# Rotating the token indexer's queries and keys in feature layout, with VectorE's shuffle in place of TensorE transposes

## Chip, cores and metric

The kernel runs on one core of one Trainium2 chip. The metric is the device time of one launch in microseconds (us), the median over repeated runs. Five engines run their own instruction streams: TensorE (PE, with its weight loads shown apart as PEld), VectorE (DVE), ScalarE (ACT), GpSimd (POOL) and SyncE (SP), whose queue here issues nearly all DMAs.

## Reference, cut to what matters

The reference is one encoder layer: RMSNorm, one input projection, two groups of attention heads, a gated output projection, a residual add. The change touches the indexer of group A, which scores keys for every query and lets each query keep its 128 best:

```python
q_i = q_i.reshape(B, S, IDX_HEADS, IDX_DIM)                       # 8 heads of 64
q_i = jnp.concatenate([rope(q_i[..., :IDX_ROPE_DIM], pos), q_i[..., IDX_ROPE_DIM:]], axis=-1)
k_i = jnp.concatenate([rope(k_i[..., :IDX_ROPE_DIM], pos), k_i[..., IDX_ROPE_DIM:]], axis=-1)
...
rel = jax.nn.relu(jnp.einsum('bqhd,bsd->bqhs', qib, k_idx))
score = jnp.einsum('bqhs,bqh->bqs', rel, wb) * idx_scale          # wb: w_i, one weight a head
```

`rope` turns the first 32 of 64 features: with halves x1, x2 of 16 features it gives x1·cos − x2·sin and x2·cos + x1·sin, an angle for each position. S is 512, the model width 1024, all values float32.

## The kernel before, in words

Every float32 operand of a matmul is split into a rounded part and a rest (`xh`, `xl` of the normed input; `wh`, `wl` of a weight chunk), and a product is three matmuls: high·high, high·low, low·high (`mm3`, L188). A weight chunk is 128 rows of a projection. `chunk` (L292) loads it (SP), ACT casts it to `wh` (L299), and POOL or DVE subtracts to `wl` (L302). The chunks stand in one list in the order of their use (L314 to L320), with three staging buffers behind the first eight chunks, so a load waits for the subtraction three chunks back. A letter per chunk says which engine subtracts: "PPPD" for the eight chunks of q_i, "P" for c_kv, "D" for c_q.

PE's order is that of the program text; that of the other engines comes from a scheduler and from explicit edges (`after`, L232; `first`, L257, which holds the casts of later chunks behind an instruction). `later` (L137) puts off a closure, such as a turn of finished rows by transposes, until so much PE time has been issued. `stream` (L342) runs several accumulations staggered by `skew` chunks, each in a PSUM bank of the tags named; the tags hold 3 (mm), 2 (tr), 2 (sc) and 1 (pv) banks.

The stretch around the change runs like this:

- The small projection (104 columns: the 32 rotary key columns of group B, then the 64 of `k_i`, then the 8 of `w_i`) accumulates feature by token in `sm_acc`, in between the first steps of q_i (L540 to L553).
- `use_small` (L456) copies it out, four transposes bring it to token layout, DVE rotates there with the table `cs32`, a second turn of four 128x128 transposes brings `k_i`, written twice side by side, back to feature layout, and `split` makes KIH and KIL.
- q_i is projected token by feature, for the token tiles 1 to 3 (tile 0 needs no scores): `tok_jobs` at L539, 3 jobs of 8 chunks of 3 matmuls, 128x512 each. `use_qi` (L566) rotates a finished tile on DVE (three operations of 128x256), and 3000 ns of PE time later four 128x128 transposes turn it, two casts on ACT and two subtractions on DVE fill the tiles QI (rounded part in one half of the partitions, rest in the other).
- `lkv` (L629) projects c_kv feature by token, 2 jobs of 8 chunks; after nine steps the index matmuls (L602, L603) come in between, two for each head and token tile, in the banks sc and tr by turns; ACT takes the relu, DVE adds it up with the weight of the head (L608, L610). Then comes c_q (`lq`, L630).
- `tables` (L425) multiplies, on POOL, the rotary tables with the gains of the head norms (TB for group B, TA for group A).

Of the kernel before, what the change touches and what calls it, by code (L numbers as in the profile page):

```python
# [88 lines left out]
def layer(ctx: ExitStack, tc: tile.TileContext, x, norm_gain, w_in, a_q_norm, a_k_norm, b_q_latent,  # L89
# [364 lines left out]
    QSUM = []  # L454

    def use_small(_, a):  # L456
        st = tmp()
        first(nc.scalar.copy(st[:104], a[:104]), KEEP_SMALL)

        def turn():  # L460
            p = psum("tr")
# [2 lines left out]
            nc.scalar.copy(sm.rearrange("p t c -> p (t c)"), p[:, :416])
            p3 = p[:, :416].rearrange("p (t c) -> p t c", t=NT)

            kid = tmp((128, NT, 128))
            k4 = kid.rearrange("p t (u d) -> p t u d", u=2)
            m = tmp((128, NT, 32))
            for u in range(2):  # L470
                nc.scalar.copy(k4[:, :, u, 32:64], p3[:, :, 64:96])
            src = p3[:, :, 32:64]
            nc.vector.tensor_tensor(halves(m), halves(src)[:, :, ::-1, :], halves(cs32[:, 1]), op=OP.mult)
            nc.vector.tensor_tensor(src, src, cs32[:, 0], op=OP.mult)
            for u in range(2):
                nc.vector.tensor_tensor(k4[:, :, u, 0:32], src, m, op=OP.add)
# [593 lines left out]
```

## Time and profile before

| what | value |
|---|---|
| median of 3 runs | 337.01 us (336.97 to 338.79) |
| the profiled execution's own time | 336.93 us |
| its span, first to last instruction | 335.2 us |
| what lies around the span | 1.7 us |
| instructions | 5486 |
| HBM read, written | 27.07 MB, 2.10 MB |

The time of an instruction in the profile is its busy time. Matmuls are pipelined, so one of 0.40 us can be followed by the next 0.23 us later: what a matmul costs is read from the distance of two starts. A number in brackets behind a row of the timeline is idle time of the engine just before, with what ended it; a row with x4 merges four instructions in a row.

### The profile page before, as it was taken

What the parts mean: (1) busy time and instruction counts of PE and PEld (TensorE: products, weight loads), DVE (VectorE), ACT (ScalarE), POOL (GpSimd) and SP (SyncE); (2) the same over time, 40 slices, a digit from 0 to 9 for tenths busy, and PEclk for the clock granted to TensorE, in tenths of its full rate; (3) what the DMA queues carried; (4) which work ended last, traced back from release to release, by engine and by line L of the source; (5) the groups of instructions that cost most, each with busy time, mean ns of one, the idle gap of its engine ahead of it and who ended that gap; (6) DMA issues with size and microseconds to landing.
All of it is one profiled execution on the core that took longest, in us unless ns stands there. A gap on an engine that the chain in (4) does not pass through costs nothing.

```text
span 335.2 us, 5486 instructions
## 1 busy us (share of the span) xinstructions
PE 327.5 (98%) x1691; PEld 274.2 (82%) x1691; DVE 261.2 (78%) x630; ACT 214.7 (64%) x530; POOL 183.7 (55%) x203
## 2 busy tenths in 40 slices
PE   7899999999999999999999999999999999999995
PEld 5788888888898988888888888888778788888884
DVE  4864779669998595778898989777997776878466
ACT  4925658683666677878877898434426988978210
POOL 3846543376899996135714579537734535745100
PEclk9999999999999999999999999999999999999999
DMA  7912344133133324014300354208977324420006
GB/s 277 356 35 62 98 119 135 45 104 95 44 93 94 101 83 131 1 36 124 77 19 1 88 140 134 80 0 191 228 178 230 91 75 141 127 64 1 2 0 250
DMA packets 28695, 34.77 MB, mean 104 GB/s; under 512 B 5357, under 2 KB 16762, under 8 KB 28666
## 3 DMA queue, kind: packets, MB, share of 16 engines
q1 hardware_dynamic: 25856, 32.45, 34.3%
q10 hardware_dynamic: 2810, 1.97, 2.3%
q8 instruction: 13, 0.21, 0.3%
q14 instruction: 16, 0.13, 0.1%
HBM read 27.07 MB, written 2.10 MB: 87 GB/s over the span
## 4 chain that ended last, share of the span: by engine, by line
PE 91%; DVE 3%; DMA 1%; issue 1%; POOL 1%; ACT 1%; SPq 0%; DVEq 0%; POOLq 0%
PE mm L130 54%; PE sc L130 12%; PE pv L130 11%; PE tr L134 6%; PE tr L130 5%; PE mm L134 2%; DVE ob L1025 2%; DMA xin<-in_x 1%; PE sc L134 1%; PE pv L134 1%; DVE xin L385 0%; POOL tmp L840 0%; POOL sml L227 0%; DVE mal L843 0%; DVE z L764 0%
## 5 line engine op out<-in xcount | busy, mean ns | idle before, releaser
L302 POOL TENSOR_TENSOR wl<-wst,wh 128x512 fp32r<-128x512 f32 (+2 forms) x80 | 100.4, 1264 | 47.9 <-ACT wh L299 43.3
L299 ACT CAST wh<-wst 128x512 fp32r<-128x512 f32 (+2 forms) x89 | 50.8, 589 | 23.7 <-DMA wst<-in_w_in 12.7
L130 PE MATMUL mm<-wh,xh 128*128 128x512 f32 x112 | 47.0, 420 | 0.0
L130 PE MATMUL mm<-wl,xh 128*128 128x512 f32 x112 | 44.4, 397 | 0.0
L130 PE MATMUL mm<-wh,xl 128*128 128x512 f32 x112 | 44.3, 395 | 0.0
L766 ACT ACTIVATE z<-z,sml 128x256 f32<-128x256 f32 (+2 forms) x64 | 35.9, 561 | 9.6 <-DVE sml L764 8.7
L795 POOL TENSOR_SCALAR z<-z,sml 128x512 f32<-128x512 f32 (+2 forms) x32 | 18.0, 561 | 42.8 <-DVE sml L791 30.5
L227 POOL TENSOR_TENSOR sml<-sml,nhalf 128x4 f32<-128x4 f32 (+2 forms) x28 | 31.6, 1130 | 14.9 <-ACT sml L918 13.7
L130 PE MATMUL mm<-xh,wh 128*128 128x512 f32 x88 | 36.7, 417 | 0.0
L130 PE MATMUL mm<-xl,wh 128*128 128x512 f32 x88 | 34.8, 395 | 0.0
L130 PE MATMUL mm<-xh,wl 128*128 128x512 f32 x88 | 34.7, 394 | 0.0
L621 DVE MAX8 m<-acc 128x8 f32<-128x512 f32 (+2 forms) x48 | 26.4, 551 | 0.0
L622 DVE MATCH_REPLACE8 acc<-m,acc 128x512 f32<-128x512 f32 (+2 forms) x48 | 25.9, 541 | 0.0
L130 PEld LDWEIGHTS mm<-wh,xl 128*128 128x128 f32 x112 | 21.1, 188 | 4.8
L130 PEld LDWEIGHTS mm<-wl,xh 128*128 128x128 f32 x112 | 21.2, 190 | 3.5 <-POOL wl L302 0.5
L130 PEld LDWEIGHTS mm<-wh,xh 128*128 128x128 f32 x112 | 21.1, 189 | 3.1 <-issue 0.2
L447 DVE TENSOR_TENSOR pl<-tr,ph 128x512 fp32r<-128x512 f32 (+1 forms) x32 | 17.6, 549 | 4.7 <-ACT ph L447 4.7
L764 DVE CUSTOM_DVE_ANT_0 z<-sc,wide,nqb 128x512 f32<-128x512 f32 (+3 forms) x32 | 17.3, 541 | 4.2 <-PE sc L130 4.0
L447 ACT CAST ph<-tr 128x512 fp32r<-128x512 f32 (+1 forms) x32 | 15.1, 472 | 8.5 <-PE tr L134 8.1
L130 PE MATMUL sc<-kl,bhl 96*128 96x512 f32 (+3 forms) x96 | 20.0, 320 | 0.0
L130 PEld LDWEIGHTS mm<-xh,wl 128*128 128x128 f32 x88 | 16.5, 188 | 4.0
L130 PEld LDWEIGHTS sc<-kl,bhl 96*128 96x128 f32 x96 | 16.7, 189 | 3.0
(248 smaller groups left out, 878.8 us busy)
## 6 DMA issues: line engine op xcount, KB each, us to landing
wst<-in_w_in SPq DMA_DIRECT2D x48, 256.0 KB, 2.7
wst<-in_w_out SPq DMA_DIRECT2D x16, 256.0 KB, 2.8
xin<-in_x SPq DMA_DIRECT2D x4, 512.0 KB, 4.8
ob<-in_x SPq DMA_DIRECT2D x8, 256.0 KB, 3.9
wst<-in_w_in SPq DMA_DIRECT2D x8, 192.0 KB, 2.4
wst<-in_w_uq SPq DMA_DIRECT2D x6, 192.0 KB, 2.6
wst<-in_w_in SPq DMA_DIRECT2D x8, 128.0 KB, 2.2
wst<-in_w_ukv SPq DMA_DIRECT2D x4, 256.0 KB, 2.8
```

The source lines that it names most:

```text
L130: nc.tensor.matmul(o, l, r, start=start, stop=stop)
L134: nc.tensor.transpose(o, i, idn)
L227: return nc.gpsimd.tensor_tensor(dst, src, nhalf[:, :src.shape[-1]], op=OP.pow)
L299: copies.append(nc.scalar.copy(h, st))
L302: i = E(eng).tensor_tensor(l, st, f32(h), op=OP.subtract)
L447: return nc.scalar.copy(h, p), nc.vector.tensor_tensor(l, p, f32(h), op=OP.subtract)
L621: nc.vector.max(m, masks[t])
L622: MR.append(nc.vector.match_replace(masks[t], m, masks[t], -3e38))
L764: m = nc.vector.tensor_tensor_reduce(z, sc[:, :n], mask(t), nq(h, t), 3e38, OP.add, OP.min, r[:, i:i + 1])
L766: e = nc.scalar.activation(z, z, AF.Exp, bias=r[:, i:i + 1], scale=-1.0, accum_out=r[:, 2 + i:3 + i])
L795: nc.gpsimd.tensor_scalar(z, z, w, 0.0, op0=OP.mult, op1=OP.add)
L1025: ADD[name, c, t] = nc.vector.tensor_tensor(o, p[:, :n], o, op=OP.add)
```

## The change

Queries and keys of the indexer never enter token layout.

- q_i is projected feature by token: `qi_jobs` makes four jobs (groups of 128 columns, two heads each) over the 384 tokens of the tiles 1 to 3, 8 chunks of 3 matmuls, 128x384 each, in the banks mm, mm, tr, sc.
- In that layout the two halves of a rotary pair lie 16 partitions apart in a block of 32. `use_qi` shuffles the bank's partitions by 16 within each block to SBUF (`stream_shuffle`, DVE), multiplies the bank in place with the cosines (DVE) and the shuffled copy with the signed sines (POOL), and adds the copy onto the bank (DVE). The casts and subtractions to QI read the bank; the 12 transposes of q_i are gone.
- `use_small` does the same with the 64 rows of `k_i`, which now lie first among the 104, and KIH and KIL are written twice from the bank; the second turn with its four transposes is gone, and the first turns only 40 rows (`w_i`, rotary keys of group B) instead of 104.
- Cosines and sines in feature layout are 1024 new columns of the constants, loaded in two DMAs of 256 KB (`turns`) on SP's queue, behind the table `cs32`. DVE's operand `turns[0]` is 1 and POOL's `turns[1]` 0 on the 32 features that do not turn.
- The subtractions of c_q's chunks go to POOL and DVE by turns. The products of `table` are put behind the last sine product on POOL. The edge that held KIL behind the last rotary sum of q_i falls away.

```diff
+    freqs = np.power(10000.0, -np.arange(16) * 2.0 / 32).astype(np.float32)
+    ang = (pos[None, :] * freqs[:, None]).astype(np.float64)
+    c, s = np.cos(ang), np.sin(ang)
+    head = np.stack([np.concatenate([c, c, np.ones((32, S))]), np.concatenate([-s, s, np.zeros((32, S))])], 1)
+    feat = np.concatenate([head, head]).reshape(128, -1).astype(np.float32)
...
+QI_SKEW = 1.99
+QI_BANK = "mm", "mm", "tr", "sc"
+QI_POOL = True
...
-        nc.sync.dma_start(wst[:, ks, 0:32], wv[:, ks, 3272:3304])
-        nc.sync.dma_start(wst[:, ks, 32:104], wv[:, ks, 2560:2632])
+        nc.sync.dma_start(wst[:, ks, 72:104], wv[:, ks, 3272:3304])
+        nc.sync.dma_start(wst[:, ks, 0:72], wv[:, ks, 2560:2632])
...
+    turns = [sb("pt2", (128, S), name=f"turns{i}") for i in range(2)]
...
-    weight("c_q", "D")
+    weight("c_q", "PD")
...
-        nc.gpsimd.tensor_tensor(dst[:, 0], raw[:, 0], g[:, None, :].to_broadcast([128, NT, d]), op=OP.mult)
+        after(nc.gpsimd.tensor_tensor(dst[:, 0], raw[:, 0], g[:, None, :].to_broadcast([128, NT, d]), op=OP.mult), SINE[-1])
...
     def use_small(_, a):
-        st = tmp()
-        first(nc.scalar.copy(st[:104], a[:104]), KEEP_SMALL)
+        st, m = tmp(), tmp()
+        first(nc.scalar.copy(st[64:104], a[64:104]), KEEP_SMALL)
+        w = sb("bq", (64, S))
+        nc.vector.stream_shuffle(w, a[0:64], [(i + 16) % 32 for i in range(32)])
+        nc.vector.tensor_tensor(a[0:64], a[0:64], turns[0][0:64], op=OP.mult)
+        nc.gpsimd.tensor_tensor(w, w, turns[1][0:64], op=OP.mult)
+        nc.vector.tensor_tensor(a[0:64], a[0:64], w, op=OP.add)
+        for u in range(2):
+            nc.scalar.copy(KIH[HALF[u]], a[0:64])
+        for u in range(2):
+            kil = nc.vector.tensor_tensor(KIL[HALF[u]], a[0:64], f32(KIH[0:64]), op=OP.subtract)
 
         def turn():
             p = psum("tr")
             for t in range(NT):
-                transpose(p[:, t * 104:t * 104 + 104], st[:104, tok(t)], ident[:104, :104])
+                transpose(p[:, t * 40:t * 40 + 40], st[64:104, tok(t)], ident[64:104, 64:104])
...
-            def turn2():
-                p = psum("tr")
-                for t in range(NT):
-                    transpose(p[:, tok(t)], kid[:, t], ident)
-                kil = split(KIH, KIL, p)[1]
-                if len(QSUM) == 3:
-                    after(kil, QSUM[2])
-            later(LAG_KI, turn2)
...
+    def qi_jobs():
+        def job(g):
+            def step(a, k):
+                h, l = wt("q_i", k)
+                mm3(a[:, :384], h[:, tok(g)], l[:, tok(g)], xh(k)[:, 128:], xl(k)[:, 128:], k == 0, k == 7)
+            return 8, step, lambda a: use_qi(g, a)
+        return [job(g) for g in range(4)]
...
-    qi_ = stream(tok_jobs("q_i", 8, xh, xl, 512, [1, 2, 3], lambda t, a: use_qi(t, a), mm3=mm3w), 3, ("mm", "mm", "pv"), 1.99)
+    qi_ = stream(qi_jobs(), 4, QI_BANK, QI_SKEW)
...
             nc.sync.dma_start(cs32, cst[:, 512:768])
+            for i in range(2):
+                nc.sync.dma_start(turns[i], cst[:, 1408 + i * S:1408 + i * S + S])
...
-    def use_qi(t, a):
-        q = tmp()
...
-        rope_mul(a3[:, :, 0:32], m, a3[:, :, 0:32], cs32, t, 8, 32)
-        QSUM.append(nc.vector.tensor_tensor(q3[:, :, 0:32], a3[:, :, 0:32], m, op=OP.add))
...
-            for h in range(4):
-                transpose(p[:, tok(h)], q[:, tok(h)], ident)
...
+    def use_qi(g, a):
+        w = sb("bq", (128, 384))
+        p = a[:, :384]
+        nc.vector.stream_shuffle(w, p, [(i + 16) % 32 for i in range(32)])
+        nc.vector.tensor_tensor(p, p, turns[0][:, 128:], op=OP.mult)
+        sine = (nc.gpsimd if QI_POOL else nc.vector).tensor_tensor(w, w, turns[1][:, 128:], op=OP.mult)
+        SINE.append(sine)
+        QSUM.append(nc.vector.tensor_tensor(p, p, w, op=OP.add))
+        for u in range(2):
+            nc.scalar.copy(QI[u][HALF[u], g], p[HALF[u]])
+        for u in range(2):
+            nc.vector.tensor_tensor(QI[u][HALF[1 - u], g], p[HALF[u]], f32(QI[u][HALF[u], g]), op=OP.subtract)
```

How the order moves on three engines. First PE, where q_i ends and c_kv begins (L134 is a transpose, `pv_355` the bank of the last q_i tile, `mm_514` that of c_kv). Before:

```order
L134 MATMUL tr_477<-ident_65,tmp_450 128x128 x4
L130 MATMUL pv_355<-wh_299,xh1_107 128x512
L130 MATMUL pv_355<-wh_299,xl1_109 128x512
L130 MATMUL pv_355<-wl_300,xh1_107 128x512
L130 MATMUL mm_514<-xh0_106,wh_310 128x512
L130 MATMUL mm_514<-xl0_108,wh_310 128x512
L130 MATMUL mm_514<-xh0_106,wl_311 128x512
L134 MATMUL tr_524<-ident_65,tmp_414 128x128 x4
L130 MATMUL mm_514<-xh0_106,wh_327 128x512
```

PE at the same place now (`tr_359` and `sc_419` are the banks of the third and fourth group of q_i, `mm_554` that of c_kv):

```order
L138 MATMUL tr_359<-xh1_109,wh_301 128x384
L138 MATMUL tr_359<-xl1_111,wh_301 128x384
L138 MATMUL tr_359<-xh1_109,wl_302 128x384
L138 MATMUL sc_419<-xh1_109,wh_295 128x384
L138 MATMUL sc_419<-xl1_111,wh_295 128x384
L138 MATMUL sc_419<-xh1_109,wl_296 128x384
L138 MATMUL sc_419<-xh1_109,wh_301 128x384
L138 MATMUL sc_419<-xl1_111,wh_301 128x384
L138 MATMUL sc_419<-xh1_109,wl_302 128x384
L138 MATMUL mm_554<-xh0_108,wh_312 128x512
L138 MATMUL mm_554<-xl0_110,wh_312 128x512
L138 MATMUL mm_554<-xh0_108,wl_313 128x512
```

The turns between the projections are gone, and c_kv follows q_i directly; from the first index matmul on PE's order is the old one. Second DVE, from the second group of q_i to the last subtraction for QI (`qi0`, `qi1`), as it stands now; `kr` is the product of the group B keys with the table TB:

```order
L584 TENSOR_TENSOR mm_323<-mm_323,bq_490 128x384
L580 STREAM_SHUFFLE bq_526<-sc_419 128x384
L581 TENSOR_TENSOR sc_419<-sc_419,turns0_98 128x384
L584 TENSOR_TENSOR tr_359<-tr_359,bq_511 128x384
L588 TENSOR_TENSOR qi0_402<-mm_323,qi0_402 64x384
L588 TENSOR_TENSOR qi1_403<-mm_323,qi1_403 64x384
L588 TENSOR_TENSOR qi0_402<-tr_359,qi0_402 64x384
L588 TENSOR_TENSOR qi1_403<-tr_359,qi1_403 64x384
L311 TENSOR_TENSOR wl_576<-wst_573,wh_575 128x384
L584 TENSOR_TENSOR sc_419<-sc_419,bq_526 128x384
L691 TENSOR_TENSOR kr_904<-sm_155,tb1_151 128x128
```

Behind these stand one more subtraction for c_q and the two subtractions of the fourth group, ahead of the first accumulation of the index. Third POOL, from the sine product of the keys (L472) to the first of the queries (L582):

```order
L311 TENSOR_TENSOR wl_296<-wst_293,wh_295 128x512
L472 TENSOR_TENSOR bq_393<-bq_393,turns1_99 64x512
L311 TENSOR_TENSOR wl_313<-wst_310,wh_312 128x256
L311 TENSOR_TENSOR wl_330<-wst_327,wh_329 128x256
L311 TENSOR_TENSOR wl_349<-wst_346,wh_348 128x256
L311 TENSOR_TENSOR wl_369<-wst_366,wh_368 128x256
L582 TENSOR_TENSOR bq_463<-bq_463,turns1_99 128x384
```

The first four subtractions of c_kv stand ahead of the first sine product of the queries; the other three sine products come, one or two chunks apart, among the rest of c_kv and the first of c_q, and all of `table` behind the last.

More of the change, by code (lines that the diff above doesn't have):

```diff
@@ L40, in constants @@
     wide = np.concatenate([np.zeros((128, 384), np.float32), mask], 1)
+    freqs = np.power(10000.0, -np.arange(16) * 2.0 / 32).astype(np.float32)
[3 more added lines that the diff above has]
+    feat = np.concatenate([head, head]).reshape(128, -1).astype(np.float32)
     return np.ascontiguousarray(
-        np.concatenate([table(64), table(32), np.eye(128, dtype=np.float32), wide], 1))
+        np.concatenate([table(64), table(32), np.eye(128, dtype=np.float32), wide, feat], 1))
 AHEAD = 8
@@ L414, in table @@
         h = d // 2
-        nc.gpsimd.tensor_tensor(dst[:, 0], raw[:, 0], g[:, None, :].to_broadcast([128, NT, d]), op=OP.mult)
+        after(nc.gpsimd.tensor_tensor(dst[:, 0], raw[:, 0], g[:, None, :].to_broadcast([128, NT, d]), op=OP.mult), SINE[-1])
         for a, b in ((0, h), (h, 0)):
-            nc.gpsimd.tensor_tensor(dst[:, 1, :, a:a + h], raw[:, 1, :, a:a + h],
-                                    g[:, None, b:b + h].to_broadcast([128, NT, h]), op=OP.mult)
+            after(nc.gpsimd.tensor_tensor(dst[:, 1, :, a:a + h], raw[:, 1, :, a:a + h],
+                                          g[:, None, b:b + h].to_broadcast([128, NT, h]), op=OP.mult), SINE[-1])
     TB = [P.tile([128, 2, NT, 32], F32, name=f"tb{i}") for i in range(2)]
@@ L462, in turn @@
             for t in range(NT):
-                transpose(p[:, t * 104:t * 104 + 104], st[:104, tok(t)], ident[:104, :104])
[L464 to L476, printed above, removed]
-            nc.scalar.activation(sm[:, :, 96:104], sm[:, :, 96:104], AF.Copy, scale=512 ** -0.5)
-            def turn2():
-                p = psum("tr")
-                for t in range(NT):
-                    transpose(p[:, tok(t)], kid[:, t], ident)
-                kil = split(KIH, KIL, p)[1]
-                if len(QSUM) == 3:
-                    after(kil, QSUM[2])
-            later(LAG_KI, turn2)
+                transpose(p[:, t * 40:t * 40 + 40], st[64:104, tok(t)], ident[64:104, 64:104])
+            p3 = p[:, :160].rearrange("p (t c) -> p t c", t=NT)
+            nc.scalar.copy(sm, p3)
+            nc.scalar.activation(sm[:, :, 0:8], sm[:, :, 0:8], AF.Copy, scale=512 ** -0.5)
         later(LAG_SMALL, turn)
@@ L564, in layer @@
     QI = [sb("qk8", (128, 4, 384), F32R, f"qi{u}") for u in range(2)]
-    def use_qi(t, a):
-        q = tmp()
-        q3 = q.rearrange("p (h d) -> p h d", h=8)
-        m = tmp((128, 8, 32))
-        a3 = a.rearrange("p (h d) -> p h d", h=8)
-        first(nc.scalar.copy(q3[:, :, 32:64], a3[:, :, 32:64]), KEEP_QI)
-        rope_mul(a3[:, :, 0:32], m, a3[:, :, 0:32], cs32, t, 8, 32)
-        QSUM.append(nc.vector.tensor_tensor(q3[:, :, 0:32], a3[:, :, 0:32], m, op=OP.add))
-        def turn():
-            p = psum("tr" if t == 1 else "sc")
-            for h in range(4):
-                transpose(p[:, tok(h)], q[:, tok(h)], ident)
-            p3 = p.rearrange("p (h c) -> p h c", h=4)
-            for u in range(2):
-                nc.scalar.copy(QI[u][HALF[u], :, tok(t - 1)], p3[HALF[u]])
-            for u in range(2):
-                a, b = QI[u][HALF[u], :, tok(t - 1)], QI[u][HALF[1 - u], :, tok(t - 1)]
-                nc.vector.tensor_tensor(b, p3[HALF[u]], f32(a), op=OP.subtract)
-        later(LAG_QI, turn)
+    def use_qi(g, a):
[10 more added lines that the diff above has]
+            nc.vector.tensor_tensor(QI[u][HALF[1 - u], g], p[HALF[u]], f32(QI[u][HALF[u], g]), op=OP.subtract)
     run(qi_)
```

9 lines of the change are left out of this document (5 added, 4 removed).

## Prediction

> **What bounds the kernel now.** I read the page first: the busy shares, the granted clock, the chain that ended last.
>
> ```profile
> PE 327.5 (98%) x1691; PEld 274.2 (82%) x1691; DVE 261.2 (78%) x630; ACT 214.7 (64%) x530; POOL 183.7 (55%) x203
> PEclk9999999999999999999999999999999999999999
> PE 91%; DVE 3%; DMA 1%; issue 1%; POOL 1%; ACT 1%; SPq 0%; DVEq 0%; POOLq 0%
> ```
>
> PE is busy for 98% of the span at the full granted clock, and the chain runs over it for 91%. A busy PE is not yet a PE without holes, so I read the stages next.
>
> ```profile
> core 0: us, PE busy (x) PEld busy (x) DVE busy (x) ACT busy (x) POOL busy (x), PEclk, DMA share, GB/s
> 15.00:36.00 21.00, 21.00 (x103) 17.09 (x103) 11.23 (x21) 9.34 (x25) 10.84 (x10) 1.00 0.26 76
> 36.00:50.00 14.00, 14.00 (x69) 11.36 (x68) 11.66 (x19) 9.27 (x20) 8.02 (x17) 1.00 0.44 119
> 50.00:130.00 80.00, 80.00 (x387) 67.95 (x386) 65.24 (x169) 53.28 (x139) 60.45 (x66) 1.00 0.32 91
> 130.00:250.00 120.00, 119.95 (x651) 100.85 (x650) 103.53 (x248) 80.27 (x195) 62.85 (x56) 1.00 0.38 92
> 250.00:305.00 55.00, 54.46 (x302) 46.02 (x301) 41.25 (x123) 45.31 (x116) 28.09 (x31) 1.00 0.39 116
> ```
>
> From 15 to 250 us PE is without a visible hole. So the time is PE's list of work plus what it waits for: PE work taken out between 15 and 50 us, where the change lies, shortens the run one for one, and a new wait of PE lengthens it one for one. Work on DVE and POOL costs only where it makes PE wait.
>
> **Part 1, the turns that go.** PE's timeline around one turn (start, busy time, what):
>
> ```profile
> 36.54 0.39 PE L130 MATMUL mm<-xh,wl 128*128 128x512 f32 x1
> 36.77 0.60 PE L134 MATMUL tr<-ident,tmp 128*128 128x128 f32 x4
> 37.12 0.48 PE L130 MATMUL mm<-xh,wh 128*128 128x512 f32 x1
> 37.44 0.40 PE L130 MATMUL mm<-xl,wh 128*128 128x512 f32 x1
> 37.68 0.40 PE L130 MATMUL mm<-xh,wl 128*128 128x512 f32 x1
> ```
>
> The four transposes hold PE from 36.77 to 37.12, 0.35 us. The matmul behind them takes 0.32 to the next start, where the one after it takes 0.24: 0.08 more. A turn costs 0.43 us. All such transposes of this stretch (34 to 41 us):
>
> ```profile
> L134 PE MATMUL tr<-ident,tmp x8: 272/273/273, 34.9 to 37.1; 128*128 128x128 f32 x8
> L134 PE MATMUL sc<-ident,tmp x8: 272/273/274, 37.9 to 40.1; 128*128 128x128 f32 x8
> ```
>
> Sixteen of one length, so four turns (three of q_i, the second of `k_i`): 4 × 0.43 = 1.72 us out.
>
> The first turn of the small projection stays, with 40 columns for 104:
>
> ```profile
> 27.55 0.52 PE L134 MATMUL tr<-ident,tmp 104*128 104x104 f32 x4
> 27.84 0.48 PE L130 MATMUL mm<-wh,xh 128*128 128x512 f32 x1
> 28.16 0.39 PE L130 MATMUL mm<-wh,xl 128*128 128x512 f32 x1
> ```
>
> It takes 0.29 us for 416 columns; by columns 160 take 0.11, by instructions still 0.29. The turn above had 512 columns in 0.35, nearly in proportion, so I take 0.12 us out, between 0 and 0.18.
>
> **Part 2, q_i in other tiles.** 72 matmuls of 512 columns become 96 of 384, the same 36,864 columns. Both widths side by side:
>
> ```profile
> 89.74 0.39 PE L130 MATMUL mm<-xh,wh 128*128 128x512 f32 x1
> ...
> 90.44 0.34 PE L130 MATMUL sc<-wh,lath 128*128 128x384 f32 x1
> ...
> 91.49 0.39 PE L130 MATMUL mm<-xh,wh 128*128 128x512 f32 x1
> ```
>
> Three of 512 take 0.70 us (89.74 to 90.44), then six of 384 take 1.05 (to 91.49): 0.233 and 0.175 each. 72 × 0.233 = 16.8 and 96 × 0.175 = 16.8: nothing.
>
> [...]
>
> **Part 3, the operands at q_i's start.** The steps are shorter, so each chunk is wanted earlier, and POOL and DVE make them no faster:
>
> ```profile
> 13.52 3.81 POOL L302 TENSOR_TENSOR wl<-wst,wh 128x512 fp32r<-128x512 f32 x3
> 18.88 3.29 DVE L538 TENSOR_TENSOR swl<-smw,swh 128x416 fp32r<-128x416 f32 x2
> 15.88 0.39 PE L130 MATMUL mm<-wh,xh 128*128 128x512 f32 x1
> 22.89 2.00 PE L130 MATMUL mm<-xh,swl 128*104 128x512 f32 x8
> ```
>
> The second chunk began at 15.88; now the first step is 0.17 shorter, so at 15.71, and its third matmul, which reads the rest, at 16.06: the second of POOL's three ends at 13.52 + 2/3 × 3.81 = 16.06. The low products of the small projection, behind nine steps, move from 22.89 to 22.89 − 9 × 0.175 = 21.31; their second half wants DVE's second instruction (done 22.17) at 21.31 + 4 × 0.23 = 22.23. Both just fit, with no room for the way of a signal. I take 0.1 us lost, between 0 and 0.3. SP's queue gets the two loads of `turns` behind that of `cs32`:
>
> ```profile
> 12.37 0.41 SPq L551 DMA_DIRECT2D cs<-cst  x1
> 13.05 0.33 SPq L295 DMA_DIRECT2D wst<-in_w_in  x1
> 28.58 4.68 SPq L295 DMA_DIRECT2D wst<-in_w_in  x5
> 36.23 0.33 SPq L427 DMA_DIRECT2D tmp<-cst  x1
> ```
>
> Two issues at the 0.68 us between these first two set the next rows back by 1.4 us, while the five loads at 28.58 wait for staging buffers anyway; and `turns` is wanted only behind the small projection, after 23 us. The load of the raw table (36.23) now stands ahead of those five; its buffer held only squares of the input norm, done long before, so it goes at once. Cost nothing; if it did wait, the c_kv loads would, and with them POOL's list in part 4.
>
> **Part 4, the long chain on DVE and POOL.** Neither a shuffle nor a sine product is in this trace; the nearest rows, by form:
>
> ```profile
> L573 DVE TENSOR_TENSOR tmp<-mm,tmp 128x256 f32<-128x256 f32 x2 | 0.8, 424 | 0.1
> L584 DVE TENSOR_TENSOR qi<-sc,qi 64x512 fp32r<-64x512 f32 x4 | 2.8, 688 | 0.1
> L302 DVE TENSOR_TENSOR wl<-wst,wh 128x384 fp32r<-128x384 f32 x5 | 3.2, 654 | 1.5 <-ACT wh L299 1.4
> L688 DVE TENSOR_TENSOR kr<-sm,tb 128x128 f32<-128x128 f32 x1 | 0.9, 909 | 0.0
> L302 POOL TENSOR_TENSOR wl<-wst,wh 128x384 fp32r<-128x384 f32 x6 | 6.1, 1019 | 0.5 <-ACT wh L299 0.5
> ```
>
> DVE on a bank takes 0.42 us for 256 columns and 0.69 for 512, so 0.56 for 384, and I price the shuffle like that. From below it is bounded by 0.42, from above by the dearest 512-column instruction of the stretch:
>
> ```profile
> 26.59 1.37 DVE L302 TENSOR_TENSOR wl<-wst,wh 128x512 fp32r<-128x512 f32 x1 [4.43 <-ACT wh L299]
> 31.15 0.74 POOL L302 TENSOR_TENSOR wl<-wst,wh 128x256 fp32r<-128x256 f32 x1 [1.20 <-ACT wh L299]
> 46.69 0.40 PE L130 MATMUL sc<-kih,qi 128*128 128x512 f32 x1
> ```
>
> [...]
>
> POOL works in order, and the first sine product of the queries stands behind the fourth subtraction of c_kv, the one at 31.15 us, which waits for ACT's cast; the change puts one more product (the keys' sine) ahead of it and moves nothing forward there. So the sine runs from 31.9 to 32.9 (1.02 us). Behind it DVE has, up to the last subtraction of the fourth group, ten instructions of 384 columns on a bank, eight half-height ones of 384 for QI, two subtractions for c_q and `kr`: 18 × 0.56 + 2 × 0.65 + 0.91 = 12.3 us, done at 45.2. All of this is hidden behind c_kv's projection until PE wants the fourth group's bank (sc) for the third index pair. That pair was at 46.69, and comes 1.74 earlier (1.72 + 0.12 − 0.1): 44.95. I take 0.3 us of wait there, between 0 and the upper case below. Who stands behind that wait on PE: everything, and PE has no room later to win it back.
>
> **Part 5, POOL's longer list.** Five sine products and four subtractions of c_q come on, about 5 × 1.02 + 4 × 1.02 = 9 us:
>
> ```profile
> 54.18 1.29 POOL L502 TENSOR_TENSOR tmp<-tmp 128x512 f32<-128x512 f32 x1 [8.63 <-ACT tmp L499]
> ```
>
> POOL idled 8.63 us ahead of this instruction, and it had waits of over 4 us earlier, so it takes them; DVE, rid of four c_q subtractions, has them back when the index sums come. Cost nothing; without that idle time four c_q rests would come up to 4 us late.
>
> **Sum.** 336.93 (the profiled execution, span 335.2 and 1.7 around it) − 1.72 − 0.12 + 0 + 0.1 + 0.3 = **335.5 us**. The profiled execution lies 0.08 under the median of 337.01, so no correction.
>
> **Rivals.**
>
> 1. *DVE's chain is late, and the turns come back as a wait* (slower than before). Place: the third index pair. It decides once the wait there passes 1.74 us, so when the chain ends after 46.7: three shuffles lie in it behind the first sine, and 0.5 us more for each does it. At 1.37 us each, 3 × 0.81 = 2.4 later, 47.6, a wait of 2.7: 336.93 − 1.74 + 2.7 = 337.9. For it: the chain is already the tightest place. Against it: bank operations keep close to their columns throughout this trace. Chance 0.13; half as late, 0.6 to 1.7 us of wait, gives 335.8 to 336.9, chance 0.2.
> 2. *A fixed price for each matmul.* Switching the kind of matmul cost 0.08 behind a turn; if each of the 24 further matmuls carried that, 1.9 us: 337.4. Against it the rows of part 2, where six in a row carry none. [...] Chance 0.03.
> 3. *No new wait at all.* The shuffle is short, the first sine comes sooner: 335.1 or, with the narrow turn at its best, 335.0. This is the near side of my forecast, and I count it there.
> 4. *More than the turns is won*, as c_q's and later stages find DVE freer: PE shows no holes that could close before 250 us, and 0.5 us from there to 305. At most 334.6; chance 0.04.
>
> **How the numbers follow.** The forecast with waits of 0 to 0.6 us, 335.0 to 335.8, has 0.6; the half-late chain 0.2, the late one 0.13, the others 0.07. The range 334.8 to 337.4 takes in the forecast, the half-late chain and the nearer part of the late one. 1% (3.4 us) is about what a measurement of this kernel can tell from no change. To be faster by that, twice the work that goes would have to go, the far end of rival 4: 0.02. Slower by that wants a wait of over 5 us on PE, the far end of rival 1, where shuffles at 1.37 us alone don't suffice: 0.04. Within it: 0.94.
>
> **What would show it.** In the profile after, 16 transposes fewer between 15 and 45 us; q_i's triples 0.52 us apart; the first index matmul near 42.6 us in place of 44.38; a shuffle at 0.45 to 0.6 us; the third index pair at about 45.2 with DVE as its releaser; from there each PE row earlier by the same amount to the end. Wrong would be: triples at over 0.55 us, PE idle of over 0.6 us between 40 and 50 us, or an end that doesn't move with the first index matmul.

## The result and the profile after

| | before | changed |
|---|---|---|
| median, range (6 runs each) | 337.11 us (336.75 to 339.3) | 342.45 us (341.74 to 343.12) |
| ratio, 95% interval | | 1.014 (1.0107 to 1.0172) |
| profiled execution, span | 336.93, 335.2 | 343.12, 341.4 |

The change makes the kernel 5.3 us slower; forecast were 335.5 us and a range to 337.4. The page of the changed kernel, the three lines with which the prediction began:

```profile
PE 328.2 (96%) x1699; PEld 277.9 (81%) x1699; DVE 267.7 (78%) x636; ACT 215.1 (63%) x528; POOL 192.7 (56%) x212
...
PEclk9899998999999999999999999999999999999999
...
PE 83%; DVE 6%; issue 3%; POOL 3%; ACT 2%; DMA 1%; SPq 0%; DVEq 0%; POOLq 0%; ACTq 0%
```

Two slices of PEclk are below full, and DVE's share of the chain has gone from 3 to 6%. The stretches, in the columns of before:

```profile
core 0: us, PE busy (x) PEld busy (x) DVE busy (x) ACT busy (x) POOL busy (x), PEclk, DMA share, GB/s
11.00:13.00 2.00, 1.72 (x9) 1.72 (x9) 1.97 (x6) 2.00 (x7) 1.82 (x4) 0.56 1.00 304
13.00:15.00 2.00, 2.00 (x13) 2.00 (x12) 1.09 (x3) 0.58 (x2) 2.00 (x3) 0.59 0.98 338
...
36.00:50.00 14.00, 11.40 (x52) 9.24 (x50) 13.11 (x19) 6.16 (x14) 12.04 (x22) 1.00 0.27 73
50.00:130.00 80.00, 78.57 (x367) 66.67 (x368) 64.78 (x163) 52.54 (x134) 56.65 (x62) 0.98 0.31 87
```

From 36 to 50 us PE, which had no hole there, is busy for 11.40 of 14.00 us, and DVE is busier than it was (13.11 for 11.66). On PE's timeline the hole is one wait:

```profile
51.43 0.47 PE L138 MATMUL sc<-kih,qi 128*128 128x512 f32 x1 [4.03 <-DVE qi L588]
...
52.64 0.63 PE L138 MATMUL pv<-xh,wl 128*128 128x512 f32 x1
53.07 0.63 PE L138 MATMUL pv<-xh,wh 128*128 128x512 f32 x1
```

It is the third index pair, where the forecast had 0.3 us of wait. A second cost stands behind it: the next matmuls come 0.43 us apart (52.64 to 53.07) instead of 0.23, until 55.62. The granted clock, 1.00 from 51 to 52 us, is 0.50 from 52.2 to 55.6 us. DVE, which is waited for, at the same time:

```profile
43.45 5.09 DVE L311 TENSOR_TENSOR wl<-wst,wh 128x384 fp32r<-128x384 f32 x1
48.57 0.57 DVE L584 TENSOR_TENSOR sc<-sc,bq 128x384 f32<-128x384 f32 x1
49.05 0.28 DVE L691 TENSOR_TENSOR kr<-sm,tb 128x128 f32<-128x128 f32 x1
49.25 0.55 DVE L311 TENSOR_TENSOR wl<-wst,wh 128x384 fp32r<-128x384 f32 x1
50.16 1.12 DVE L588 TENSOR_TENSOR qi<-sc,qi 64x384 fp32r<-64x384 f32 x2 [0.36 <-ACT qi L586]
```

One subtraction of c_q takes 5.09 us; the same instruction takes 0.55 six us later. And POOL:

```profile
40.02 0.18 POOL L440 TENSOR_TENSOR gcol<-gcol 64x1 f32<-64x1 f32 x1
40.17 1.00 POOL L311 TENSOR_TENSOR wl<-wst,wh 128x384 fp32r<-128x384 f32 x1
...
47.14 0.99 POOL L311 TENSOR_TENSOR wl<-wst,wh 128x384 fp32r<-128x384 f32 x1
51.56 1.01 POOL L311 TENSOR_TENSOR wl<-wst,wh 128x384 fp32r<-128x384 f32 x1 [3.44 <-ACT wh L308]
```

POOL runs the fourth sine product, TB, TA and a c_q subtraction without a pause, to 47.14 + 0.99 = 48.13 us. DVE's instruction, which reads two SBUF tiles (`wst`, `wh`), ends at 43.45 + 5.09 = 48.54, 0.41 later. DVE's instructions that read a bank and one SBUF tile run at their usual 0.55 to 0.57 beside POOL.

### The profile page after: what moved, and what is told of

The parts are those of the page before. It is cut to its first block, busy times and chain, and to the rows that moved or that the text cites. A ratio compares the mean times of both kernels' runs of the same rounds, so it can differ in the third digit from the quotient of the medians.

```text
span 341.4 us, 5518 instructions
## 1 busy us (share of the span) xinstructions
PE 328.2 (96%) x1699; PEld 277.9 (81%) x1699; DVE 267.7 (78%) x636; ACT 215.1 (63%) x528; POOL 192.7 (56%) x212
## 4 chain that ended last, share of the span: by engine, by line
PE 83%; DVE 6%; issue 3%; POOL 3%; ACT 2%; DMA 1%; SPq 0%; DVEq 0%; POOLq 0%; ACTq 0%
PE mm L138 49%; PE sc L138 12%; PE pv L138 8%; PE tr L138 6%; PE tr L142 6%; DVE ob L1028 2%; PE mm L142 2%; DMA xin<-in_x 1%; POOL wl L311 1%; DVE qi L588 1%; PE sc L142 1%; POOL sml L235 1%; PE pv L142 0%; DVE xin L394 0%; POOL tmp L843 0%
## 5 line engine op out<-in xcount | busy, mean ns | idle before, releaser
L311 POOL TENSOR_TENSOR wl<-wst,wh 128x512 fp32r<-128x512 f32 (+2 forms) x84 | 104.2, 1248 | 52.7 <-ACT wh L308 50.1
L798 POOL TENSOR_SCALAR z<-z,sml 128x512 f32<-128x512 f32 (+2 forms) x32 | 18.0, 563 | 42.6 <-DVE sml L794 30.2
L138 PE MATMUL mm<-xh,wh 128*128 128x512 f32 (+1 forms) x104 | 42.0, 404 | 0.0
L138 PE MATMUL mm<-wh,xh 128*128 128x512 f32 x96 | 40.6, 423 | 0.1
L138 PE MATMUL mm<-xl,wh 128*128 128x512 f32 (+1 forms) x104 | 40.2, 387 | 0.0
L138 PE MATMUL mm<-xh,wl 128*128 128x512 f32 (+1 forms) x104 | 40.2, 387 | 0.0
L138 PE MATMUL mm<-wl,xh 128*128 128x512 f32 x96 | 38.0, 396 | 0.0
L138 PE MATMUL mm<-wh,xl 128*128 128x512 f32 x96 | 37.9, 395 | 0.0
L138 PEld LDWEIGHTS mm<-xh,wl 128*128 128x128 f32 x104 | 19.5, 188 | 4.2 <-POOL wl L311 0.2
L138 PEld LDWEIGHTS mm<-xh,wh 128*128 128x128 f32 x104 | 19.6, 188 | 1.7
L138 PEld LDWEIGHTS mm<-xl,wh 128*128 128x128 f32 x104 | 19.6, 189 | 1.5
```

Of the source, the lines that this page charges most:

```text
L138: nc.tensor.matmul(o, l, r, start=start, stop=stop)
L311: i = E(eng).tensor_tensor(l, st, f32(h), op=OP.subtract)
L798: nc.gpsimd.tensor_scalar(z, z, w, 0.0, op0=OP.mult, op1=OP.add)
```

## The experiments

**Theory 1 (T1):** DVE's instruction that reads two SBUF tiles is held as long as POOL works on without a pause. **Theory 2 (T2):** DVE's list is simply too long for the 8 us from the end of q_i. **Theory 3 (T3):** the instruction waits for its input, the c_q chunk's load or cast. All times are beside runs of the kernel before on the same chip (medians 336.85 to 338.21). The first four runs change one of the two sides of theory 1 each.

### e1: the TA products taken out of POOL's run

The products of TA and their load move behind POOL's subtractions for c_q:

```diff
     def tables():
-        raw = tmp((128, 2, NT, 64))
-        nc.sync.dma_start(raw, cst[:, 0:512])
...
-        for i in range(2):
-            table(TA[i], raw, ga[:, i], 64)
+    def tables_a():
+        raw = tmp((128, 2, NT, 64))
+        nc.sync.dma_start(raw, cst[:, 0:512])
+        SINE.append(subs[-1])
+        for i in range(2):
+            table(TA[i], raw, ga[:, i], 64)
...
     weave((take(lq, I2), I2), (ix, 24 - I1))
+    tables_a()
```

> The products of group A's table (TA) and their load come only behind the last c_q subtraction on POOL; all else is the changed kernel. Theory 1 (VectorE's instruction with two SBUF operands is held as long as GpSimd works on without a pause): GpSimd's run that ended at 48.1 us now ends at 44.1 us or, with one c_q subtraction behind it, at 45.1 us; the c_q subtraction on VectorE that took 5.09 us takes 1.2 to 2.2 us; the third index pair waits 0 to 1.1 us in place of 4.0, TensorE's clock does not fall, and the time is 336.5 to 337.7 us. Theory 2 (VectorE's list of new instructions is simply too long): nothing of that list changes, 342 us. Theory 3 (the c_q chunk's load or cast is late): 342 us, or a little less.

Measured: 339.28 us (338.35 to 341.07), ratio 1.0059 (1.0034 to 1.0083). DVE's and PE's rows:

```profile
43.52 2.10 DVE L311 TENSOR_TENSOR wl<-wst,wh 128x384 fp32r<-128x384 f32 x1
```
```profile
PE tr L142 <- POOL tmp L504: 1.5, 1, 1.5
PE sc L138 <- DVE qi L591: 1.0, 1, 1.0
```

POOL's run now ends at 45.21 (its last c_q subtraction 44.20 + 1.01), DVE's instruction at 45.62: again 0.41 behind. The wait at the third pair falls from 4.0 to 1.0. The second line is a price of the new place: a latent sum on POOL comes late behind the moved products, and PE waits 1.5 for it. So the time is 1.6 us above the 337.7 that theory 1 allowed, while DVE's instruction took the 1.2 to 2.2 us that it foretold.

### e3: the TA products twice

```diff
-        for i in range(2):
+        for i in (0, 1, 0, 1):
             table(TA[i], raw, ga[:, i], 64)
```

> The four groups of TA products on GpSimd are computed twice (same values, work doubled). Theory 1: GpSimd's run without a pause grows by up to 3.2 us, and so do the c_q subtraction on VectorE (5.09 to about 8 us) and the wait of the third index pair (4.0 to about 7): about 345.5 us; less if GpSimd pauses for a cast between the two sets. Theories 2 and 3: 342 us, the subtraction stays at 5.1 us, since nothing that VectorE, the casts or the loads do has changed.

Measured: 343.92 us (343.24 and 344.6), ratio 1.0187 (1.0119 to 1.0256), a wait of 5.5 at the third pair. DVE, then the last instruction of POOL's run and the one behind its pause:

```profile
43.33 6.60 DVE L311 TENSOR_TENSOR wl<-wst,wh 128x384 fp32r<-128x384 f32 x1
```
```profile
48.66 0.85 POOL L426 TENSOR_TENSOR ta<-tmp,ga 128x128 f32<-128x128 f32 x2
53.00 1.01 POOL L311 TENSOR_TENSOR wl<-wst,wh 128x384 fp32r<-128x384 f32 x1 [3.48 <-ACT wh L308]
```

POOL's run ends at 49.51, DVE's instruction at 49.93. Only one of the two added sets fell into the run, the other came behind the pause, so the growth is half of what was expected. Not a row of DVE's list has changed, so theory 2 can't give this.

### e5: all subtractions of c_q on POOL

```diff
-    weight("c_q", "PD")
+    weight("c_q", "P")
```

> All c_q subtractions go to GpSimd; VectorE's order is the changed kernel's without them, so the product for group B's keys (0.28 us alone, two SBUF operands) is the first such instruction ahead of the last subtractions for QI. Theory 1: that product is now the one that is held, from about 44.5 us until GpSimd pauses at 48.1 us or later (one more c_q subtraction stands in its list), so 3.5 to 5 us; the third index pair waits 3 to 5 us: 341 to 343 us. Theory 2: 1.1 us shorter, 341 us, with the product at 0.28 us. Theory 3 (the c_q chunk on VectorE is the trouble, by its load or cast): gone, 336.5 us.

Measured: 342.42 us (341.57 and 343.27), ratio 1.0143 (1.0072 to 1.0214), a wait of 4.5. Now `kr` is the first on DVE with two SBUF tiles:

```profile
43.66 6.60 DVE L691 TENSOR_TENSOR kr<-sm,tb 128x128 f32<-128x128 f32 x1
```
```profile
47.22 2.89 POOL L311 TENSOR_TENSOR wl<-wst,wh 128x384 fp32r<-128x384 f32 x3
```

Four subtractions fewer on DVE save nothing; `kr`, 0.28 us long and without a load of its own, is held to the end of POOL's run (50.11). Theories 2 and 3 fall.

### e4: QI's last subtractions ahead of the instructions that are held

```diff
+        if eng == "D" and QSUB:
+            after(i, QSUB[-1])
...
-            nc.vector.tensor_tensor(QI[u][HALF[1 - u], g], p[HALF[u]], f32(QI[u][HALF[u], g]), op=OP.subtract)
+            i = nc.vector.tensor_tensor(QI[u][HALF[1 - u], g], p[HALF[u]], f32(QI[u][HALF[u], g]), op=OP.subtract)
+        if g == 3:
+            QSUB.append(i)
...
-    nc.vector.tensor_tensor(kr, src, TB[1][:, 0], op=OP.mult)
+    after(nc.vector.tensor_tensor(kr, src, TB[1][:, 0], op=OP.mult), QSUB[-1])
```

> The changed kernel with VectorE's order turned: the two c_q subtractions and the product for group B's keys stand behind the last subtraction for QI. Theory 1: the c_q subtraction, now at about 46 us, is still held until GpSimd pauses at 48.1 us (about 2 us in place of 0.55), but the fourth group is done at 46.3 us and the third index pair waits for nothing: 336.2 to 336.8 us. Theory 2: the list ahead of the index is shorter by 2 x 0.55 + 0.28 = 1.4 us only, so a wait of 2.6 us stays and the clock still falls: about 340.5 us. Theory 3 (load or cast late): the late chunk no longer holds the fourth group, 336.5 us, and the subtraction on VectorE takes 0.55 us wherever its cast is done.

Measured: 336.92 us (336.18 to 339.75), ratio 1.0003 (0.9976 to 1.003).

```profile
44.69 2.68 DVE L311 TENSOR_TENSOR wl<-wst,wh 128x384 fp32r<-128x384 f32 x1
```
```profile
PE tr L138 <- DVE acc L617: 0.5, 1, 0.5
```

The third pair waits no more, and the 5 us are back. The c_q subtraction is still held, to POOL's end (46.95; it ends 47.37), and now the index sums behind it are late: PE waits 0.5 at 56.05, and the 0.7 to 1.0 us that it was ahead of before from 46 to 54 us are gone there.

### e6: the held instruction and POOL's run kept apart

As e4, and the TA products with their load stand behind POOL's first latent sum, ahead of a pause that it has anyway:

```diff
-            nc.gpsimd.tensor_tensor(sqs[0], sqs[0], sq, op=OP.add)
+            SINE.append(nc.gpsimd.tensor_tensor(sqs[0], sqs[0], sq, op=OP.add))
+            if sqs is ckvs:
+                tables_a()
```

> DVE's order as in e4 (QI's last subtractions ahead of c_q's and kr), and the TA products with their load stand behind POOL's first latent sum (53.6 us in e4), where POOL then waited over 5 us for ACT. Theory 1 (a DVE instruction that reads two SBUF tiles is held while POOL works on without a pause): POOL's run ends near 44 instead of 46.95, so DVE's first c_q subtraction, 2.68 us in e4, takes under 1.3; the wait of 0.53 at 56.05 (tr, releaser DVE's accumulation) is gone, and the turns stay won. In e4's profile PE was 0.89 to 0.71 ahead of before at 49 us and nothing at 56; so 336.9 - 0.8 = 336.1, with 335.6 to 336.5 as bounds. Theory 2 (DVE's list is simply too long there): the list is the same as in e4, so the wait at 56 stays, 336.9. If POOL's c_q subtractions or the second latent sum come late behind the TA products (as in e1): a PE wait with releaser POOL, up to 1.5, 337.5.

Measured: 335.55 us (335.34 to 337.26), ratio 0.9956 (0.9938 to 0.9975).

```profile
44.43 0.56 DVE L311 TENSOR_TENSOR wl<-wst,wh 128x384 fp32r<-128x384 f32 x1
44.91 0.28 DVE L699 TENSOR_TENSOR kr<-sm,tb 128x128 f32<-128x128 f32 x1
```

With POOL idle since 43.32 (its subtraction 42.31 + 1.01), both take their usual time. The kernel is 1.3 us faster than before: this is what the change is worth when nothing is held.

### e7: the first turn with all its rows

```diff
-        first(nc.scalar.copy(st[64:104], a[64:104]), KEEP_SMALL)
+        first(nc.scalar.copy(st[:104], a[:104]), KEEP_SMALL)
...
-                transpose(p[:, t * 40:t * 40 + 40], st[64:104, tok(t)], ident[64:104, 64:104])
+                transpose(p[:, t * 104:t * 104 + 104], st[:104, tok(t)], ident[:104, :104])
```

> The kernel of e6, but the small projection's turn takes all 104 rows again from partition 0 (104x104 instead of 40x40 from partition 64; 416 columns out, of which the copy reads the same 160). If the narrow turn's price (0.37 us for 160 columns in the changed kernel, against 0.29 for 416 before) comes from where it sits in its rows, the wide one takes 0.29 here and the run is 0.1 to 0.2 us shorter than e6. If it comes from the place in the program (what stands around it), the wide one takes 0.37 or more here, and the time is e6's or slightly above.

Measured: 335.51 us (335.18 to 337.5), ratio 0.9961 (0.9939 to 0.9982), the same as e6 within what runs differ by. The rows tell them apart; first e6, then e7:

```profile
26.40 0.34 PE L138 MATMUL mm<-xh,wl 128*128 128x384 f32 x1
26.66 0.44 PE L142 MATMUL tr<-ident,tmp 40*128 40x40 f32 x4
...
27.32 0.34 PE L138 MATMUL mm<-xl,wh 128*128 128x384 f32 x1
```
```profile
26.56 0.34 PE L138 MATMUL mm<-xh,wl 128*128 128x384 f32 x1
26.74 0.52 PE L142 MATMUL tr<-ident,tmp 104*128 104x104 f32 x4
...
27.30 0.34 PE L138 MATMUL mm<-xl,wh 128*128 128x384 f32 x1
```

From the start of the matmul ahead to that of the second one behind, the narrow turn takes 0.92 us, the wide one 0.74: 0.18 us more for 160 columns than for 416. Whether that is the 40 rows or their place from partition 64 on, e7 doesn't part.

### e8 and e9: both kernels once more

> The kernel before, profiled once more. The changed kernel's profile had the granted clock at 0.56 to 0.59 from 11 to 15 us, behind a PE idle of 1.73 us before the third x tile's turn, which set q_i's start back by 1.83 us; before's one profile had 1.57 us idle there and full clock. If that is from run to run, this profile may show the dip as well, and then its span is near 337; if it belongs to the change, it shows none, span 335.2.

> The changed kernel, profiled once more. If the dip of the clock at 11 to 15 us is from run to run, this profile may come without it, and is then 1.5 to 1.9 us shorter than the 343.1 of the first; the DVE instruction of 5.09 us at 43.5 and the PE wait of about 4 us at the third index pair must be there in either case.

Measured: 338.94 and 341.24 us. A window at the start, of the kernel before, then of the changed one (PEclk is the third number from the end):

```profile
11.00:13.00 2.00, 1.91 (x10) 1.91 (x11) 1.95 (x6) 2.00 (x7) 1.82 (x4) 0.59 0.97 322
```
```profile
11.00:13.00 2.00, 2.00 (x18) 2.00 (x19) 1.85 (x5) 2.00 (x7) 1.88 (x4) 1.00 0.98 324
```

This time the kernel before has the low clock (0.59, and 0.55 in the next two us), and the changed one has not. So these 1.9 to 2 us belong to neither: they come and go from run to run, and explain most of the ranges of both. They also bear on the 5.3 us of the medians. By the mean granted clock (0.990 with the dip as in the first profile, 0.995 without it as in e9) four of the six runs of the changed kernel had the dip; by their times (338.79 and 339.3 against 336.75 to 337.2) two of the six of before. Without it the change costs 4.3 us (e9 against the profiled execution of before) to 4.9 us (341.74 and 341.96 against the mean of the other four).

### e2, e10 and e11: when does DVE get in?

Theory 1 as it stands doesn't explain the kernel before: there `kr` (0.91) and the c_q subtraction (0.81) got in beside the very same TA products. The rows of before, POOL and DVE:

```profile
37.53 1.43 POOL L302 TENSOR_TENSOR wl<-wst,wh 128x256 fp32r<-128x256 f32 x2 [4.62 <-ACT wh L299]
```
```profile
41.59 0.91 DVE L688 TENSOR_TENSOR kr<-sm,tb 128x128 f32<-128x128 f32 x1
```

Three runs vary what stands around them. e2 drops the edges that put the tables behind the sine products:

```diff
-        after(nc.gpsimd.tensor_tensor(dst[:, 0], raw[:, 0], g[:, None, :].to_broadcast([128, NT, d]), op=OP.mult), SINE[-1])
+        nc.gpsimd.tensor_tensor(dst[:, 0], raw[:, 0], g[:, None, :].to_broadcast([128, NT, d]), op=OP.mult)
...
```

> The changed kernel without the edges that put the norms' tables behind the sine products; POOL then has TB and TA ahead of the third and fourth sine product, and DVE has kr ahead of all of QI's subtractions. Theory 1 (held while POOL works on without a pause): POOL has work from about 36 to 46 us without a pause; kr, at about 39, is held for most of that, some 5 us or more, and everything of QI behind it; PE waits at the first or the third index pair, 4 to 7 us in all, 342 to 345. If DVE gets in after one POOL instruction, as in the kernel before: kr and c_q's subtraction 0.9 each, the fourth sine done near 45.5 and QI's last pair at 48, a wait of about 1 us, 338.

e10 has the four sine products of the queries on DVE (`QI_POOL = False`):

> The queries' four sine products on DVE instead of POOL (POOL 4 us shorter, DVE 2.2 us longer), all else as in the changed kernel; the tables still stand behind the fourth sine. Theory 1: POOL's run without a pause is then TB, TA and a c_q subtraction, 2.1 + 3.1 + 1.0 us, and it begins where DVE's last sine ends; the c_q subtraction behind it on DVE is held for most of these 6 us, a PE wait of 3 to 5 at the third pair, 341 to 343.5: the shorter POOL list saves next to nothing. Theory 2 (DVE's own list is too long): 2.2 us more than the changed kernel, 344.5 or more. If POOL's length itself were the cost: 338.

e11 is the kernel before with three more shuffles of 128 columns that nothing reads:

```diff
         QSUM.append(nc.vector.tensor_tensor(q3[:, :, 0:32], a3[:, :, 0:32], m, op=OP.add))
+        nc.vector.stream_shuffle(SPARE, a[:, :128], [(i + 16) % 32 for i in range(32)])
```

> The kernel before with three added shuffles on DVE (128 columns of each q_i bank to a spare tile, read by nothing). Before, kr (0.91) and the c_q subtraction (0.81) got in after one POOL instruction although POOL worked on; in the changed kernel they did not. If the shuffle leaves DVE in a state in which it loses to POOL, one of the two takes 2 to 4 us here, until POOL's pause near 45.6, and PE waits at the third index pair by 1 to 3 us, 338 to 340. If not, they take 0.8 to 0.95 again, 337.0 to 337.5 (or up to 339 with the dip of the clock at the start).

Measured: e2 338.43 us (337.77 to 340.53), ratio 1.0047 (1.0021 to 1.0073); e10 336.97 us (336.58 to 337.15), 0.9991 (0.9977 to 1.0006); e11 338.45 (one run, with the low clock at the start: 0.61 and 0.53). In none of the three is DVE held: the c_q subtraction takes 0.69, 1.07 and 0.81. So the expectation from theory 1 failed in e2 and e10, and the shuffle is not the cause. The rows of e10, DVE and POOL:

```profile
42.39 1.07 DVE L311 TENSOR_TENSOR wl<-wst,wh 128x384 fp32r<-128x384 f32 x1
```
```profile
42.31 0.74 POOL L424 TENSOR_TENSOR ta<-tmp,ga 128x256 f32<-128x256 f32 x1
43.01 1.20 POOL L426 TENSOR_TENSOR ta<-tmp,ga 128x128 f32<-128x128 f32 x2
```

Here DVE gets in when POOL changes from one instruction to the next, and POOL pays: 1.20 us for a pair that takes 0.87 elsewhere. So POOL's work is not enough; something decides whether a change of instruction lets DVE in. (e2 loses its time in another way: its fourth sine product comes late, PE waits 2.0 us at the index. e10, with the sine products in DVE's list, still has a wait of 1.0 at the third pair.)

### e12, e13 and e14: which break in POOL's work it takes

What differs is how long POOL has worked since it last stood still. e12 adds, behind the first product of each table, a product of one column that reads what was just written, a self-wait; this also moves two c_q subtractions up on POOL:

```diff
+        SINE.append(nc.gpsimd.tensor_tensor(DRAIN, dst[:, 0, 0, 0:1], dst[:, 0, 0, 1:2], op=OP.mult))
```

> The changed kernel with one more POOL instruction of one column behind the first product of each table, which reads what POOL has just written, so that POOL must finish that write before it goes on (a self-wait). DVE got in beside the same tables in the kernel before, in e2 and in e10, and never in the changed kernel, e1, e3, e4 and e5. If it is POOL's instructions following each other without any self-wait that shut DVE out, the c_q subtraction (5.09 us) gets in at the first such point and takes under 1.3; PE's wait at the third index pair falls from 4 to under 1, and the time to 336 to 338. If a self-wait of this length doesn't let DVE in, it is held to POOL's first true pause, which here is a wait for ACT's cast of the third c_q chunk, 3 to 5 us, and the time is 340 to 343.

e13 keeps the changed kernel's order and puts a memset, which waits for nothing, at the same four places:

```diff
+        main = nc.gpsimd.tensor_tensor(dst[:, 0], raw[:, 0], g[:, None, :].to_broadcast([128, NT, d]), op=OP.mult)
...
+        SINE.append(nc.gpsimd.memset(BREAK.pop(), 1.0))
+        after(SINE[-1], main)
```

> The changed kernel, the order on every engine kept, with a memset of one column, which waits for nothing, behind the first product of each of the four tables. If any small instruction that reads no tile lets DVE in (before and e2 have a memset just ahead of the places where DVE got in), the c_q subtraction takes under 1.3 at 43.5, PE's wait at the third index pair is under 1, and the time 335.5 to 337. If it takes a self-wait or a pause, the subtraction is held to POOL's pause near 48.5, 5 us, and the time is 341 to 343.

e14 keeps the order too, with one memset and one self-wait ahead of TB, behind the fourth sine product:

```diff
+        m = nc.gpsimd.memset(DRAIN, 1.0)
+        after(m, SINE[-1])
+        SINE.append(nc.gpsimd.tensor_tensor(DRAIN, DRAIN, DRAIN, op=OP.mult))
```

> The changed kernel, the order kept, with one memset and one self-wait of POOL ahead of the first table, behind the fourth sine product, some 1.2 us and two or three instructions before DVE's c_q subtraction asks. If what counts is how long POOL has worked since its last break (DVE got in where that was up to 1.6 us, and not where it was 3.2 us or more), the subtraction gets in at the next change, under 1.3, and the time is 335.5 to 337. If the break must come while DVE is asking, it is held 5 us, and the time is 341 to 343.

Measured:

| run | us | ratio | c_q subtraction on DVE | PE's wait at the third pair |
|---|---|---|---|---|
| e12 | 335.48 (335.27 to 337.19) | 0.9947 (0.9924 to 0.997) | 0.86 | none shown |
| e13 | 342.43 (341.51 to 342.89) | 1.0123 (1.0078 to 1.0167) | 5.23 | 4.2 |
| e14 | 335.66 (334.9 to 336.63) | 0.9934 (0.9908 to 0.9959) | 0.83 | 0.4 |

The rows of e14, DVE and POOL:

```profile
41.42 0.83 DVE L311 TENSOR_TENSOR wl<-wst,wh 128x384 fp32r<-128x384 f32 x1
...
42.76 0.80 DVE L695 TENSOR_TENSOR kr<-sm,tb 128x128 f32<-128x128 f32 x1
```
```profile
40.09 0.09 POOL L438 MEMSET drain<- 128x1 f32 x1
40.26 0.19 POOL L440 TENSOR_TENSOR drain<-drain 128x1 f32<-128x1 f32 x1
40.41 0.46 POOL L424 TENSOR_TENSOR tb<-cs,gb 128x128 f32<-128x128 f32 x1
...
41.80 0.92 POOL L426 TENSOR_TENSOR tb<-cs,gb 128x64 f32<-128x64 f32 x2
```

e14 differs from the changed kernel by two instructions of one column on POOL, 0.3 us long together, and is 6.8 us faster than it by the medians (and as much faster than e13, which ran beside it). POOL's list isn't shorter, DVE's is the same; all that is new is a self-wait of POOL 1.2 us before DVE asks. It makes POOL stand still for 0.08 us: the memset ends at 40.09 + 0.09 = 40.18, the product that waits for it begins at 40.26. Memsets alone (e13) leave no such gap, and do nothing. So the cause is settled that far: **in the changed kernel POOL, working on for some 5 us without standing still, keeps DVE's two-tile instruction out at every change of its instructions, up to its next pause; shortly after a stop (0.08 us long in e12 and e14) it lets DVE in at the next change.**

How long POOL has worked is read from its rows. While it works on, a row begins a little before the end of the one ahead. Its last stop ahead of the held instruction, in the changed kernel:

```profile
38.15 0.11 POOL L439 MEMSET gcol<- 128x1 f32 x1
38.35 0.74 POOL L311 TENSOR_TENSOR wl<-wst,wh 128x256 fp32r<-128x256 f32 x1
39.05 1.02 POOL L582 TENSOR_TENSOR bq<-bq,turns 128x384 f32<-128x384 f32 x1
```

POOL stands still from 38.26 to 38.35, and not at the `gcol` product of 40.02, which begins before the sine product ahead of it ends (39.05 + 1.02 = 40.07). From the stop to DVE asking it is 43.45 − 38.35 = 5.10 us. Counted in this way, fourteen profiles fall into two groups. It is 5.1 to 5.2 us in the changed kernel, e1, e3, e5, e9 and e13, and 7.6 in e4, all held. It is 4.1 in the two profiles of before (37.53 to 41.59), 4.3 in e11, 4.8 in e2, 1.2 in e14, 0.7 in e12 and 0.2 in e10, all let in. In e14 without the self-wait it would have been 41.42 − 36.33 = 5.1. Where a first instruction of DVE got in, later ones did too (in e10 up to 43.85, 5.1 us behind POOL's pause).

The number of POOL's instructions since the stop doesn't separate the groups (9 to 15 where DVE is held, 10 and 11 in before, e11 and e2), nor does the moment within POOL's instruction at which DVE asks (0.29 us behind its start in e4, held; 0.20 in e11 and 0.40 in e2, let in). So the profiles fit a limit between 4.8 and 5.1 us, but this is read off afterwards: no run moved that time step by step, and what sets the limit stays open. Nor does a run show why POOL's work holds DVE's instruction up: a subtraction of c_q took 0.56 us on DVE with POOL idle (e6), 0.69 to 1.07 where it was let in beside POOL (e2, e10, e11, e12, e14 and the kernel before), and 2.10 (e1) to 6.60 (e3) where it was held.

## Why the prediction was wrong, step by step

The sum of before's profiled execution and e9's, which both have full clock at the start, closes. The start of the same c_kv matmul, then the third pair and what follows it, before, then e9 (before's third pair, at 46.69, is in the prediction):

```profile
40.10 0.48 PE L130 MATMUL pv<-xh,wh 128*128 128x512 f32 x1
...
48.31 0.39 PE L130 MATMUL pv<-xh,wl 128*128 128x512 f32 x1
```
```profile
38.91 0.40 PE L138 MATMUL pv<-xh,wh 128*128 128x512 f32 x1
...
49.56 0.77 PE L138 MATMUL sc<-kih,qi 128*128 128x512 f32 x1 [3.98 <-DVE qi L588]
...
52.69 0.45 PE L138 MATMUL pv<-xh,wl 128*128 128x512 f32 x1
```

PE is 40.10 − 38.91 = 1.19 us ahead behind the turns, and 49.56 − 46.69 = 2.87 behind at the third pair: 4.06 lost. The seven steps from 49.56 to 52.69 take 3.13, before 1.62 (46.69 to 48.31): 1.51 lost to the clock. 336.93 − 1.19 + 4.06 + 1.51 = 341.3; e9 measured 341.24.

- **The step that failed: part 4, the cost of the two-tile instructions in DVE's chain** ("two subtractions for c_q and `kr`: ... 2 × 0.65 + 0.91", in which the c_q subtraction was priced by a mean and `kr` by one row), with part 5's "Cost nothing" for POOL's longer list. The two were costed each by itself. In fact the one decided the other: POOL's list, grown to a run of 9.8 us without a stop (38.35 to 48.13), kept a 0.55 us instruction out, so that it took 5.09. Two rows of before were signs of it that the prediction quoted without asking: `kr` took 0.91 for 128 columns, where it takes 0.28 with POOL idle (e6), and the 1.37 that rival 1 used as a bound for the shuffle was a two-tile subtraction beside POOL, whose twin took 0.68 (the two have a mean of 1.03).
- **The place was right.** The third index pair, released by DVE, as the prediction and its first rival had it. But the rival made the shuffles late (1.37 us each), and they took 0.59 to 0.60 each, at the upper end of the 0.45 to 0.6 that was foretold (the 0.45 no run shows); the bank operations took 0.55 to 0.57, priced at 0.56. So the wait came where the rival had it, and not for its reason.
- **The chain's own length was right.** With DVE let in (e12) the chain ends at 43.85 + 1.12 = 44.97; forecast 45.2. The third pair there starts at 45.13; forecast 45.2.
- **Part 1, the turns.** Four turns at 0.43 are not contradicted, but the narrow turn is 0.18 dearer, not 0.12 cheaper (e6, e7). The first index matmul, forecast near 42.6, starts at 43.10 in e9, 1.28 ahead of before's 44.38.
- **Part 2.** The matmuls of 384 columns stand in proportion but for 1%: in e7 45 of them from 28.18 to 36.12, 0.1764 each, and c_kv's behind them 0.2335; 96 × 0.1764 − 72 × 0.2335 = 0.1 us. Nothing like 1.9 us shows, and rival 2 falls.
- **Part 3.** The third matmul of the second chunk does come 0.1 late (e7: 16.31 to 16.59, 0.28 in place of 0.18), as taken.
- **The sum without the failed step:** −1.72 + 0.18 + 0.1 + 0.1 = −1.34. e6, e7, e12 and e14 are 1.3 to 2.6 us under before by the medians (some runs of before with the dip at the start among them, most beside e14). In the traces the matmul that stands at 90.44 in before comes at 89.15 in e6, 89.11 in e7 and 88.77 in e12; counted from q_i's first matmul (14.95 in before, 14.93, 15.17, 14.85) PE is 1.3 to 1.6 us ahead there. So the forecast of 335.5 holds for the change with POOL's run broken, not for the change as it is.
- **The other rivals.** Rival 3, no new wait, is nearly what e12 shows (the third pair comes 0.2 late); the changed kernel as it is doesn't reach it. Of rival 4 nothing clear shows: from 50 us to the end PE's lead over before grows by 0.2 to 0.6 us in e6, e7 and e12, and the two profiles of before drift apart by up to 0.7 on the same stretch.
- **What was not in the prediction at all:** the clock behind the wait (1.5 us), so that a wait of 4.0 cost 5.6. The prediction asked for a wait of over 5 us to be slower by 1%, since it took a wait one for one.

## What to carry to other kernels

Work moved to GpSimd is not free because GpSimd is idle nearly half the time (it was busy for 55% of the span of before, and the change cost 5.3 us): look at what VectorE does with two SBUF operands beside it (here it was held for up to 6.3 us, e5), and at how long GpSimd would then run without standing still (some 5 us were too long here). Where such a VectorE instruction lies ahead of something TensorE waits for, put it behind (e4, 336.92 us for the changed kernel's 342.45), put GpSimd's work elsewhere (e6, 335.55), or break GpSimd's run with one tiny self-wait shortly before (e14, 335.66). An instruction that takes three times its usual time in one place of the profile (here `kr`, 0.91 us for 0.28) is to be explained before it is used as a price.
